# Turning C's queries and keys by 32x32 blocks through memory in a two-layer decoder trunk, with edits to the order of copies, loads and residuals

## The chip, the cores and the metric

One core of a Trainium2 chip runs the whole kernel. Its engines work at the same time, each on its own queue of instructions in program order: TensorE (PE in the profile, PEld its weight loads), VectorE (DVE), ScalarE (ACT), GpSimd (POOL) and SyncE (SP), which here only issues transfers. The metric is the device time of one execution in microseconds (us).

## The reference

Two layers act on a sequence of 256 tokens with 1024 channels, all in float32:

```python
h = h + 0.5 * swiglu(rms_norm(h, g1), w_gate1, w_up1, w_down1)       # D_FF = 2816
u = rms_norm(h, gm);  P = u @ w_in                                   # one wide projection, split by columns
h = h + concat(o_A, o_B, o_C) @ w_out
h = h + 0.5 * swiglu(rms_norm(h, g2), w_gate2, w_up2, w_down2)
```

Group A has 4 query heads on one key head, and each query keeps 64 keys that an indexer scores; with 256 tokens group B (4 heads) is plain causal attention. Both norm queries and keys per head and rotate them. Group C, which the change touches, has 8 heads of 64 channels without rotation, and adds a running sum of log forget gates:

```python
cq = rms_norm(cq, c_q_norm);  ck = rms_norm(ck, c_k_norm)            # per head of 64
s  = cq @ ck.T / 8 + c_sum[query] - c_sum[key]                       # keys up to the query
o_C = softmax(s) @ cv * sigmoid(cg)
```

## The kernel before, in words

**Products.** A float32 product is made of three at full rate: each operand is split into a rounded high part (`h`) and the rest (`l`), and `mm3` adds h·h, h·l and l·h. Weights stream in tiles of 128x1024 that SP fetches (`Weights.load`, L214). `W.pump` splits one tile: ACT casts the high part (`wh`, L273), DVE subtracts for the low one (`wl`, L277). Ten raw tiles and eight split ones can be held. A tile's fetch is issued as soon as an older raw tile has been split, unless `W.hold` is set; `W.free(n)` lifts that and issues up to n at once.

**Feed-forward.** `ffn` runs the hidden columns in chunks of 512. Chunks 2 and 4 go through `seven`, a Strassen-like scheme with seven products of halves in place of eight, whose extra sums are made of copies of PSUM: `keep` (L645) is an ACT copy of a bank that TensorE goes on to write, and `V.tensor_tensor(u4, z, u4)` (L665) reads another such bank. `stepped()` stands between the parts; it runs what is due and pumps two weight tiles. Hidden chunks are turned by DVE in 32x32 blocks (`to_memory`, L474), written to memory, and read back so that the blocks lie in transposed places (`from_memory`, four transfers, L479). The last six rows of w_down are used in `tail` (from L836): for each of four quarters q it finishes `acc[q]`, adds it to the trunk (`residual`, L490) and sends half of the next layer norm's input through memory (`nxt.send`, tile `xd`); `nxt.fetch` reads it back (tile `xT`) and `nxt.rest` splits it (ACT L447, DVE L448). The other half is turned by TensorE (`norm.half`, `turn`, L418).

**Mixer.** The columns of w_in come in eight chunks of four units each, in the order iq, ib, b, a, ck, cq, cv, cg; a unit is 12 matmuls of TensorE. After unit n everything registered by `at_step` with a number up to n runs, sorted by that number, then one tile is pumped. For C, ACT evacuates `ck` and `cq` from PSUM to one SBUF tile (`wide`) and squares them; DVE sums the squares (`c_sums`). At step 25.36 one POOL power takes the root for 32 columns (`head_rs`, L394), and POOL scales the four tiles (`scale_heads`, L947); the gains of both norms are multiplied into cq by POOL (L1228). Group A's selection runs beside it on DVE: eight `topk` rounds at the odd steps from 17 to 31, then `amask` (L1091 to L1095) at step 32. POOL adds the causal mask to the forget rows (L1137).

**A and C heads.** Then AC_ORDER, a list written out by hand, sets the order of all that is left: `s` scores of a pair of heads, `m` mask and row maximum (DVE), `e` exponentials (ACT), `d`/`D` division (DVE or ACT), `f` turning the probabilities on TensorE with an ACT copy out of PSUM, `v` values, `o` output, `q` a half of a w_out product, `w` a pump, `a` a mask add, `T`/`t` turns through memory. `g` is the step of the change: `c_T` turns a pair of C heads by four TensorE transposes of each layer's cq and ck (L1436) and copies the bank to SBUF (ACT, L1437); there are four a layer.

Of the kernel before, what the change touches and what calls it, by code (L numbers as in the profile page):

```python
# [14 lines left out]
ALU = mybir.AluOpType  # L15
# [3 lines left out]
P = 128  # L19
S = 256  # L20
D = 1024
# [15 lines left out]
HELD = 6  # L37
OUT_TAIL = 3
AC_ORDER = """
g2.4 g0.5 s0.01 m0 s1.23 m3 e0 e3 s2.45 D0 q g1.0 a0 m4 m2 e2 q q D3 f0.3 a1 a3 m1 e1 s3.42 s4.01 f3.3  # L40
m5 e4 a2 m6 d2 q g3.5 d1 f2.3 q e5 m7 f1.5 m8 D4 s5.32 t m10 v0.0 w o0 e10 q q q e6 f4.3 q d5 m11 d10
e11 q f5.0 D11 m9 v1.3 T5 o1 v2.2 e8 e7 q D6 w d7 q o2 q e9 q d8 q f6.0 d9 q q w q f7.1 f8.3 f9.2 w v3.0
o3 v5.1 v4.3 o4 w q q
""".split()
# [251 lines left out]
def kernel(ctx: ExitStack, tc: tile.TileContext, x, xt, weights, small, const, out):  # L296
# [184 lines left out]
    def tokens(o, q, hid, w, start, stop, cols=slice(0, 512)):  # L481
# [2 lines left out]
        mm3(o, [h[:, t * P:(t + 1) * P] for h in hid], [v[:, 0, 512 * c + cols.start:512 * c + cols.stop] for v in w],  # L484
            start, stop)

    def residual(q, ps, factor, cols=slice(0, 512)):
        t, c = q % 2, q // 2
        d = trunk[:, t, 512 * c + cols.start:512 * c + cols.stop]
        V.scalar_tensor_tensor(d, ps, factor, d, op0=ALU.mult, op1=ALU.add)  # L490
        return d


    def ffn(norm, nxt, aside=None, first=False):
# [43 lines left out]
            ts = slice(t * P, (t + 1) * P)  # L538
            mm3(ps[t], (norm.h[:, k, ts], norm.l[:, k, ts]), [v[:, k % 2] for v in w], k == 0, k == KT - 1)

        def unit(ps, u):
            w = W.take()
            for k in (2 * u, 2 * u + 1):
                for t in range(2):
                    part(ps, k, w, t)

        def gate(ps, t, n):
            a = tmp(n)
# [79 lines left out]
        def seven(c):  # L628

            def piece(part, t, half):  # L630
                return [part[:, 4 * half + k, t * P:(t + 1) * P] for k in range(4)]

            def form(ps, x, start, stop=False, last=False):
                hs, ls = x if isinstance(x, tuple) else forms[x]
                for u in range(2):
                    w = W.take()
                    for k in range(2):
                        n = 2 * u + k
                        mm3(ps, (hs[n], ls[n]), [v[:, k] for v in w], start and n == 0, stop and n == 3)
                    if not (last and u):  # L640
                        stepped()

            def keep(ps):
                s = tmp(512)
                A.copy(s, ps)  # L645
                return s

            own = lambda t, half: (piece(norm.h, t, half), piece(norm.l, t, half))
            n_down = 1 if c == NC - 1 else 2
            y = bank("gu")  # L650
            form(y, own(0, 0), True)
            s1 = keep(y)
            x = bank("gu")
            form(x, own(0, 1), True, True)
            z = bank("gu")
            form(z, "f3", True)
            form(y, "f2", False, last=True)
            u2 = keep(y)
            stepped()
            for i in range(n_down):  # L660
                down(4 * c - 4 + i)
            V.tensor_tensor(s1, x, s1, op=ALU.add)
            form(y, "f1", False)
            u4 = keep(y)
            V.tensor_tensor(u4, z, u4, op=ALU.add)  # L665
            for i in range(n_down):
                down(4 * c - 4 + n_down + i)
            W.hold = c < NC - 1
            form(y, "f4", False, True)
            W.hold = True  # L670
            a0 = gate([s1, None], 0, 512)
            V.scalar_tensor_tensor(a0, y, minus_r[:, 0:1], a0, op0=ALU.mult, op1=ALU.mult)
            sc = memory(4, "hd")
            to_memory(sc, 0, a0, 4)
            form(z, own(1, 1), False, True, True)
            V.tensor_tensor(u2, z, u2, op=ALU.add)
            a1 = gate([None, u2], 1, 512)
            V.scalar_tensor_tensor(a1, u4, minus_r[:, 1:2], a1, op0=ALU.mult, op1=ALU.mult)
            to_memory(sc, 1, a1, 4)
            last = c == NC - 1  # L680
            if c == at_seven[-1]:
                forms.clear()
                W.home = None
            after(HID_AT, back(4 * c, 4, sc))
            W.free(2 if last else 4)
            W.hold = last
            stepped()
# [75 lines left out]
        for c in range(NC):  # L763
# [4 lines left out]
                continue  # L768
            ps = [bank("gu") for _ in range(2)] if c else g0
            for u in range(0 if c else 2, 4):  # L770
                unit(ps, u)
                if u < 3:
                    stepped()
            if c == 0:
                if first:
                    W.low()
                    norm.sums_T(xT[0])
                A.activation(minus_r, norm.r, AF.Copy, scale=-1.0)
            a = [gate(ps, t, 512) for t in range(2)]
            stepped()  # L780
# [38 lines left out]
            up(a, ps[t][:, S:], t)  # L819
            to_memory(sc, t, a, 2)  # L820
        split = back(4 * NC, 2, sc)
        W.free()
        stepped()
        stepped()
        for k in range(4 * NC - 6, 4 * NC - 4):
# [5 lines left out]
    def tail(acc, rhs, ks, factor, make_norm, late=None, early=()):  # L831
# [12 lines left out]
        if late:  # L844
# [4 lines left out]
            part(2, ks[:1])  # L849
            ahead = [2, 2, 1, 0]  # L850
        if early:
            part(0, ks[:-2])
            early[0]()
            W.pump()
            part(1, ks[:-2])
            for q in range(4):
# [2 lines left out]
                    nxt.half(0, 1)  # L859
                if q == 3:  # L860
                    W.hold = True
                    nxt.rest()
                residual(q, acc[q], factor)
                if q < 2:
                    nxt.send(q, 2, 2)
                else:
                    nxt.send(q - 2, 8 - n_far, n_far)
                nxt.squares(q % 2, q // 2)
                if q == 1:
                    nxt.fetch(2, 2)  # L870
                if q == 2:
                    W.pump()
            W.pump()
# [38 lines left out]
    G.memset(eighth, HD ** -0.5)  # L912

    def mixer(l, norm, nxt):
        room = wide().rearrange("p (n h d) -> p n h d", n=4, h=8)
        cq, ck = ([room[:, 2 * i + t] for t in range(2)] for i in range(2))
        va = [at.tile([P, 8, HD], F32, name=f"va{t}", tag=f"va{t}") for t in range(2)]
        side, count = [], itertools.count()
# [290 lines left out]
        def c_sums(i, dst, ps, when):  # L1209
# [8 lines left out]

            at_step(when, sums)

        def post_ck(ps):
            c_sums(0, ck, ps, 20.76)

        def post_cq(ps):
            c_sums(1, cq, ps, 24.83)
            for t in range(2):
                q = cq[t]
                G.tensor_tensor(q, q, gc[:, None, :].to_broadcast([P, 8, HD]), op=ALU.mult)  # L1228

            def c_norm():  # L1230
                rs = head_rs(c_ss.rearrange("p i t h -> p (i t h)"), 32, "c")
                for t in range(2):
                    for i, d in enumerate((ck, cq)):
                        x = d[t]
                        scale_heads(x, x, rs[:, 16 * i + 8 * t:16 * i + 8 * t + 8])

            at_step(25.36, c_norm)

        hr = sm.tile([P, 2], F32, name="hr", tag="hr")
        at_step(18.32, lambda: V.tensor_scalar(hr, norm.r, 0.5, None, op0=ALU.mult))  # L1240
# [4 lines left out]

        def post_cg(ps):
            spare = xp.tile([P, 4096], F32, name="spare", tag="xhl")
            st["cT"] = spare[:, :2048].rearrange("p (h c s) -> p h c s", h=4, c=2)
            st["sg"] = spare[:, 2048:3072].rearrange("p (i m r) -> p i m r", i=8, m=4)
            st["fmask"].append(spare[:, 3072:3840].rearrange("p (h c) -> p h c", h=2))  # L1250
            st["gate"] = [tmp(512) for _ in range(2)]
# [6 lines left out]
        def run_heads(hs, qk, take, emit=None):  # L1258
            pj, pt, op, sums, bs = {}, {}, {}, {}, {}

            def scores(i):
# [3 lines left out]
                    return  # L1265
                q, k = qk(kind, h)
                bs[i], bs[i + 1] = take(), take()
                for cols, qs, ks in ((slice(0, P), slice(0, P), slice(0, P)),
                                     (slice(P, 3 * P), slice(P, S), slice(0, S))):
                    products((bs[i], bs[i + 1]), cols, q[:, qs], k[:, ks], cols.start == 0)  # L1270

            def masks(i):

# [42 lines left out]
            def flip_pair(i):  # L1316

                d = tab.rearrange("p a b t d -> p (a b t d)")[:, :6 * P]
                blocks([pj.pop(2 * i + e) for e in range(2)], 3, "pd", d.rearrange("p (i x) -> p i x", i=8))
                d = d.rearrange("p (e i b c) -> p e i b c", e=2, i=4, b=3)  # L1320
                for e in range(2):
                    x = d[:, e].rearrange("p i b c -> p b i c")
# [92 lines left out]

        halves = out_halves()

        cT = st["cT"]

        given, banks = [], {}  # L1420

        def take():
# [5 lines left out]
                banks[i] = bank("gu")  # L1428
            return banks[i]

        def c_T(j, copy):

            b = take()
            for c, src in enumerate((cq, ck)):
                for t in range(2):
                    T.transpose(b[:, c * S + t * P:c * S + (t + 1) * P], src[t][:, 2 * j:2 * j + 2], ident)  # L1436
            copy(cT[:, j], b.rearrange("p (c s) -> p c s", c=2))  # L1437

        def blocks(tiles, n, name, to):
            sc = memory(n, name)  # L1440
            for t, x in enumerate(tiles):
                to_memory(sc, t, x, n)
            from_memory(sc, to, nc.sync)

        def turn_gate(_):
            blocks(st["gate"], 4, "gd", st["sg"].rearrange("p i m r -> p i (m r)"))

        def qk_ac(kind, h):
            if kind == "A":
                return st["aqT"][:, h // 2], st["akT"][:, 0]  # L1450
            return cT[:, h // 2, 0], cT[:, h // 2, 1]

        hs = [("A", h) for h in range(4)] + [("C", h) for h in range(8)]
        scores, masks, exps, divide, flip, flip_pair, values, outT = run_heads(hs, qk_ac, take)
        run = dict(q=lambda i: next(halves), w=lambda i: W.pump(), m=masks, e=exps, d=divide, D=lambda i: divide(i, True),
                   T=flip_pair, t=turn_gate,
                   s=lambda i: scores(2 * i), f=flip, F=lambda i: flip(i, V.tensor_copy),
                   g=lambda i: c_T(i, A.copy), G=lambda i: c_T(i, V.tensor_copy),
                   v=lambda i: values(2 * i + 1),
                   o=lambda i: outT(i)(), a=st["add"])  # L1460
        for word in AC_ORDER:
# [67 lines left out]
```

## Time and profile before

| | us |
|---|---|
| median of 3 runs | 979.85 (979.56 to 980.37) |
| the profiled execution, whole | 980.02 |
| its span, first to last instruction | 978.3 |
| PE busy in the span | 970.5 |
| DVE busy | 822.3 |
| ACT busy | 611.2 |
| POOL busy | 167.2 |

The span leaves 1.7 us of the execution outside. Matmuls overlap, so an engine that reads as busy can still lose a slot; where that matters the start times of neighbouring instructions are compared. A matmul with 512 columns starts 0.23 us after the one before when nothing is missing.

### The profile page before, as it was taken

What the parts mean: (1) busy time and instruction counts of PE and PEld (TensorE: products, weight loads), DVE (VectorE), ACT (ScalarE), POOL (GpSimd) and SP (SyncE); (2) the same over time, 40 slices, a digit from 0 to 9 for tenths busy, and PEclk for the clock granted to TensorE, in tenths of its full rate; (3) what the DMA queues carried; (4) which work ended last, traced back from release to release, by engine and by line L of the source; (5) the groups of instructions that cost most, each with busy time, mean ns of one, the idle gap of its engine ahead of it and who ended that gap; (6) DMA issues with size and microseconds to landing.
All of it is one profiled execution on the core that took longest, in us unless ns stands there. A gap on an engine that the chain in (4) does not pass through costs nothing.

```text
span 978.3 us, 13761 instructions
## 1 busy us (share of the span) xinstructions
PE 970.5 (99%) x4608; PEld 801.0 (82%) x4608; DVE 822.3 (84%) x1284; ACT 611.2 (62%) x1024; POOL 167.2 (17%) x190
## 2 busy tenths in 40 slices
PE   9999999999999999999999999999999999999998
PEld 8878878888878888887878888788888788888877
DVE  6999698689987799879679987976899877998794
ACT  6747475567876656547465654756677865575552
POOL 0000002187530000000000000031867200000000
PEclk9999999999999999999999999999999999999999
DMA  9878877675555687768777767877546547687661
GB/s 359 307 196 333 280 257 220 230 263 167 177 192 157 250 228 249 259 195 311 247 276 229 204 243 253 292 234 235 218 155 220 176 146 274 183 300 267 187 240 60
DMA packets 105495, 226.68 MB, mean 232 GB/s; under 512 B 20928, under 2 KB 50896, under 8 KB 105424
## 3 DMA queue, kind: packets, MB, share of 16 engines
q1 hardware_dynamic: 101936, 213.95, 63.0%
q0 software_dynamic: 2304, 8.39, 4.8%
q10 hardware_dynamic: 1184, 3.46, 1.2%
q8 instruction: 36, 0.59, 0.2%
q14 instruction: 35, 0.29, 0.1%
HBM read 208.44 MB, written 17.33 MB: 231 GB/s over the span
## 4 chain that ended last, share of the span: by engine, by line
PE 86%; DVE 5%; DMA 5%; ACT 3%; issue 1%; SPq 1%; ACTq 0%; POOL 0%; DVEq 0%; POOLq 0%
PE ps_gu L383 58%; PE ps_acc L383 25%; DMA xd<-tmp 2%; DVE wl L277 2%; ACT wh L273 2%; DMA hT<-hd 1%; DMA xT<-xd 1%; SPq L479 1%; DVE tmp L474 1%; DMA hd<-tmp 1%; PE ps_gu L1310 1%; PE ps_acc L978 1%; DVE trunk L490 1%; ACT hh L565 0%; DVE tmp L553 0%
## 5 line engine op out<-in xcount | busy, mean ns | idle before, releaser
L383 PE MATMUL ps_gu<-wh,xhl 128*128 128x512 f32 (+2 forms) x1600 | 494.6, 386 | 1.1 <-ACT xhl L447 1.0
L277 DVE TENSOR_TENSOR wl<-raw,wh 128x1024 fp32r<-128x1024 f32 (+2 forms) x340 | 406.5, 1231 | 10.7 <-ACT wh L273 10.3
L273 ACT CAST wh<-raw 128x1024 fp32r<-128x1024 f32 (+2 forms) x340 | 341.0, 1039 | 62.6 <-PE ps_acc L383 20.0
L383 PEld LDWEIGHTS ps_gu<-wh,xhl 128*128 128x128 f32 x1600 | 298.6, 188 | 62.0 <-DVE tmp L665 1.9
L383 PE MATMUL ps_gu<-wl,xhl 128*128 128x512 f32 (+2 forms) x800 | 306.2, 384 | 0.1
L383 PEld LDWEIGHTS ps_gu<-wl,xhl 128*128 128x128 f32 x800 | 150.3, 188 | 28.5 <-DVE wl L277 0.5
L383 PE MATMUL ps_acc<-wh,hh 128*128 128x512 f32 (+1 forms) x352 | 136.6, 388 | 0.0
L383 PE MATMUL ps_acc<-wh,hl 128*128 128x512 f32 (+1 forms) x352 | 136.3, 387 | 0.0
L383 PE MATMUL ps_acc<-wl,hh 128*128 128x512 f32 (+1 forms) x352 | 136.3, 387 | 0.0
L273 ACT CAST wh<-wide 128x1024 fp32r<-128x1024 f32 x48 | 50.0, 1053 | 86.8 <-DVE wide L244 52.5
L242 POOL DMA_DIRECT2D raw<-in_weights_dram x16 | 14.3, 893 | 374.9 <-DVE wide L244 255.2
L383 PEld LDWEIGHTS ps_acc<-wh,hl 128*128 128x128 f32 x352 | 66.1, 188 | 13.5
L383 PEld LDWEIGHTS ps_acc<-wh,hh 128*128 128x128 f32 x352 | 66.1, 188 | 13.5
L383 PEld LDWEIGHTS ps_acc<-wl,hh 128*128 128x128 f32 x352 | 66.1, 188 | 13.4
L277 DVE TENSOR_TENSOR wl<-wide,wh 128x1024 fp32r<-128x1024 f32 x48 | 57.5, 1212 | 5.3 <-ACT wh L273 5.1
L565 ACT CAST hh<-hT 128x256 fp32r<-128x256 f32 x88 | 29.4, 404 | 37.6 <-DMA hT<-hd 37.6
L553 DVE SCALAR_TENSOR_TENSOR tmp<-ps_gu,y_n,tmp 128x512 f32<-128x512 f32 (+1 forms) x32 | 21.3, 667 | 33.7 <-PE ps_gu L383 28.0
L566 DVE TENSOR_TENSOR hl<-hT,hh 128x256 fp32r<-128x256 f32 x88 | 32.0, 424 | 19.0 <-ACT hh L565 19.0
L394 POOL TENSOR_TENSOR y_n<-msq,minus_half 128x2 f32<-128x2 f32 x6 | 7.7, 1288 | 209.1 <-ACT wh L273 153.2
L244 DVE TENSOR_TENSOR wide<-wide,raw 128x1024 f32<-128x1024 f32 x32 | 39.1, 1222 | 0.6
L474 DVE STREAM_TRANSPOSE tmp<-tmp 128x512 f32<-128x512 f32 (+1 forms) x52 | 34.6, 668 | 1.7
L383 PE MATMUL ps_gu<-wh,fp 128*128 128x512 f32 x96 | 33.6, 390 | 0.8 <-ACT tmp L645 0.8
(259 smaller groups left out, 1095.7 us busy)
## 6 DMA issues: line engine op xcount, KB each, us to landing
raw<-in_weights_dram SPq DMA_DIRECT2D x324, 512.0 KB, 5.4
hd<-tmp SPq DMA_DIRECT2D x40, 256.0 KB, 2.0
hT<-hd SPq DMA_DIRECT2D x80, 128.0 KB, 2.6
raw<-in_weights_dram POOLq DMA_DIRECT2D x16, 512.0 KB, 6.6
raw<-in_weights_dram SPq DMA_DIRECT2D x8, 384.0 KB, 4.3
raw<-in_weights_dram SPq DMA_DIRECT2D x8, 336.0 KB, 5.0
raw<-in_weights_dram SPq DMA_DIRECT2D x8, 256.0 KB, 4.5
fmask<-fd ACTq DMA_DIRECT2D x2, 768.0 KB, 8.0
```

The source lines that it names most:

```text
L242: self.nc.gpsimd.dma_start(self.part(*unit), self.kept(rs[0], *unit[1:]), accum_op=ALU.add)
L244: self.nc.vector.tensor_tensor(self.part(*unit), *(self.part(r, *unit[1:]) for r in rs), op=ALU.add)
L273: self.nc.scalar.copy(hv, src)
L277: (engine or self.nc.vector).tensor_tensor(lv, self.srcs[self.n_low], hv.bitcast(F32), op=ALU.subtract)
L383: T.matmul(o, l, r, start=start, stop=stop, skip_group_check=True)
L474: V.transpose(o.rearrange("p (j b c) -> p b j c", j=4, b=n), x.rearrange("p (b j c) -> p b j c", b=n, j=4))
L479: (other if other and j > 1 else eng).dma_start(to[32 * j:32 * j + 32], sc[:, j].rearrange("(i r) x -> r i x", r=32))
L490: V.scalar_tensor_tensor(d, ps, factor, d, op0=ALU.mult, op1=ALU.add)
L553: V.scalar_tensor_tensor(a, u, norm.r[:, t:t + 1], a, op0=ALU.mult, op1=ALU.mult)
L565: A.copy(by(hh), x)
L566: V.tensor_tensor(by(hl), x, by(hh).bitcast(F32), op=ALU.subtract)
L978: T.transpose(ps[:, i * S + t * P:i * S + (t + 1) * P], xs[t][:, (j + i) * P:(j + i + 1) * P], ident)
```

## The change

Queries and keys of C no longer pass TensorE's transposes. `c_turn` sends a tile pair through memory by 32x32 blocks, in the way that hidden chunks go, back into the same part of `wide`. Keys go first: gains into ck, their root (16 columns) at step 21.0, their turn at 24.9. Queries: root at 24.84, turn at 27.9, with weight fetches held from 25.95 until the turn has been issued. Scores read the keys as they lie, with 32-wide runs; the queries of two pairs at a time are copied into order by ACT (`g0`, `g1`). In the feed-forward part the copy out of PSUM comes ahead of the pumps beside it, the first layer's sums of squares are issued half a unit earlier, fetches are held in the tail until the first half of the next norm is on its way, and the last quarter's residual and send come ahead of `nxt.rest`.

```diff
-g2.4 g0.5 s0.01 m0 s1.23 m3 e0 e3 s2.45 D0 q g1.0 a0 m4 m2 e2 q q D3 f0.3 a1 a3 m1 e1 s3.42 s4.01 f3.3
-m5 e4 a2 m6 d2 q g3.5 d1 f2.3 q e5 m7 f1.5 m8 D4 s5.32 t m10 v0.0 w o0 e10 q q q e6 f4.3 q d5 m11 d10
+g0 s0.01 m0 s1.23 m3 e0 e3 s2.45 D0 q g1 a0 m4 m2 e2 q q D3 f0.3 a1 a3 m1 e1 s3.42 s4.01 f3.3
+m5 e4 a2 m6 d2 q d1 f2.3 q e5 m7 f1.5 m8 D4 s5.32 t m10 v0.0 w o0 e10 q q q e6 f4.3 q d5 m11 d10
...
+    def turned(tiles, n, name, to):
+        sc = memory(n, name)
+        for t, x in enumerate(tiles):
+            to_memory(sc, t, x, n)
+        from_memory(sc, to, nc.sync)
@@ unit; the call of the first layer's first chunk gives between=6
+                if k == between:
+                    norm.sums_T(xT[0])
@@ seven
-                    if not (last and u):
+                    if not last or u < 2 - last:
                         stepped()
-            form(y, own(0, 0), True)
+            form(y, own(0, 0), True, last=True)
             s1 = keep(y)
+            stepped()
-            form(y, "f2", False, last=True)
+            form(y, "f2", False, last=2)
             u2 = keep(y)
+            stepped()
             stepped()
-            form(y, "f1", False)
+            form(y, "f1", False, last=True)
             u4 = keep(y)
             V.tensor_tensor(u4, z, u4, op=ALU.add)
+            stepped()
@@ ffn after the last hidden chunk, and tail
-        W.free()
+        W.free(4)
+        W.hold = nxt is not None
...
                 if q == 3:
                     W.hold = True
-                    nxt.rest()
                 residual(q, acc[q], factor)
...
+                if q == 3:
+                    nxt.rest()
                 nxt.squares(q % 2, q // 2)
                 if q == 1:
                     nxt.fetch(2, 2)
+                    W.free(2)
@@ mixer
+        def c_norm(i, d, tag):
+            rs = head_rs(c_ss[:, i].rearrange("p t h -> p (t h)"), 16, tag)
+            for t in range(2):
+                scale_heads(d[t], d[t], rs[:, 8 * t:8 * t + 8])
+        def c_turn(i, d, name):
+            to = wide_room[:, 1024 * i:1024 * i + 1024].rearrange("p (i x) -> p i x", i=8)
+            turned([x.rearrange("p h d -> p (h d)") for x in d], 4, name, to)
+            return to.rearrange("p i (m r) -> p m i r", m=4)
         def post_ck(ps):
             c_sums(0, ck, ps, 20.76)
+            for t in range(2):
+                k = ck[t]
+                G.tensor_tensor(k, k, gc[:, None, :].to_broadcast([P, 8, HD]), op=ALU.mult)
+            at_step(21.0, lambda: c_norm(0, ck, "ck"))
+            at_step(24.9, lambda: st.update(ckT=c_turn(1, ck, "kd")))
         def post_cq(ps):
             c_sums(1, cq, ps, 24.83)
-            for t in range(2):
-                q = cq[t]
-                G.tensor_tensor(q, q, gc[:, None, :].to_broadcast([P, 8, HD]), op=ALU.mult)
-            def c_norm():
-                rs = head_rs(c_ss.rearrange("p i t h -> p (i t h)"), 32, "c")
-                for t in range(2):
-                    for i, d in enumerate((ck, cq)):
-                        x = d[t]
-                        scale_heads(x, x, rs[:, 16 * i + 8 * t:16 * i + 8 * t + 8])
-            at_step(25.36, c_norm)
+            at_step(24.84, lambda: c_norm(1, cq, "cq"))
+            at_step(25.95, lambda: setattr(W, "hold", True))
+            at_step(27.9, lambda: st.update(cqT=c_turn(0, cq, "qd")))
+            at_step(27.9, lambda: W.free(2))
-        def c_T(j, copy):
-            b = take()
-            for c, src in enumerate((cq, ck)):
-                for t in range(2):
-                    T.transpose(b[:, c * S + t * P:c * S + (t + 1) * P], src[t][:, 2 * j:2 * j + 2], ident)
-            copy(cT[:, j], b.rearrange("p (c s) -> p c s", c=2))
+        def c_pairs(j):
+            two = slice(2 * j, 2 * j + 2)
+            A.copy(c_q[:, two].rearrange("p m (i r) -> p m i r", i=8), st["cqT"][:, two])
```

## Rows read from the trace of the kernel before

**Rows 1.** The page, part 1: busy time, share, instructions of each engine.
```profile
PE 970.5 (99%) x4608; PEld 801.0 (82%) x4608; DVE 822.3 (84%) x1284; ACT 611.2 (62%) x1024; POOL 167.2 (17%) x190
```
**Rows 2.** Waits of PEld: waiting group <- released by: us in total, times, longest.
```profile
PEld ps_gu L383 <- ACT tmp L645: 3.4, 5, 1.3
...
PEld ps_gu L383 <- DVE tmp L665: 1.9, 4, 0.5
PEld ps_gu L383 <- ACT xhl L447: 1.8, 2, 1.2
PEld ps_acc L418 <- DVE trunk L490: 1.4, 2, 0.9
...
PEld ps_gu L383 <- DVE wl L277: 0.5, 1, 0.5
```
**Rows 3.** Timeline of PE at three stalls: start, duration, what, [idle before <-releaser].
```profile
68.29 0.39 PE L383 MATMUL ps_gu<-wh,fpT 128*128 128x512 f32 x1
69.52 0.50 PE L383 MATMUL ps_gu<-wh,fp 128*128 128x512 f32 x1 [0.84 <-ACT tmp L645]
69.86 0.40 PE L383 MATMUL ps_gu<-wl,fp 128*128 128x512 f32 x1
...
493.33 0.50 PE L383 MATMUL ps_gu<-wh,xhl 128*128 128x512 f32 x1 [0.74 <-ACT xhl L447]
...
670.91 0.44 PE L418 MATMUL ps_acc<-ident,trunk 128*128 128x128 f32 x2 [0.70 <-DVE trunk L490]
```
**Rows 4.** Chain of waits between the second and third feed-forward: start, us, what.
```profile
482.46 6.53 DMA xd<-tmp
...
495.57 1.96 DMA xd<-tmp
```
**Rows 5.** Timeline of SP ahead of the first of these writes: start, us, transfers, count.
```profile
474.03 5.85 SPq L214 DMA_DIRECT2D raw<-in_weights_dram  x8
```
**Rows 6.** Chain of waits, first transposes of layer one's A/C stage.
```profile
276.46 0.87 PE ps_acc L1436 x8
```
**Rows 7.** Timeline of DVE, end of the first mixer's projection to the gate's turn.
```profile
266.49 1.21 DVE L277 TENSOR_TENSOR wl<-raw,wh 128x1024 fp32r<-128x1024 f32 x1
...
267.96 1.73 DVE L277 TENSOR_TENSOR wl<-raw,wh 128x1024 fp32r<-128x1024 f32 x1
...
273.58 2.69 DVE L1093 SCALAR_TENSOR_TENSOR amask<-score,cst 128x128 f32<-128x128 f32 x2
...
278.32 0.35 DVE L1284 CUSTOM_DVE_ANT_0 tmp<-ps_gu,amask,minus_a 128x128 f32<-128x128 f32 x1 [0.52 <-PE ps_gu L383]
...
286.70 1.28 DVE L474 STREAM_TRANSPOSE tmp<-tmp 128x512 f32<-128x512 f32 x2
```
**Rows 8.** Timeline of POOL, same stretch.
```profile
253.52 1.97 POOL L394 TENSOR_TENSOR y_a<-ssa,minus_half 128x10 f32<-128x10 f32 x1 [13.18 <-DVE sums L1300]
...
260.57 6.37 POOL L394 TENSOR_TENSOR y_c<-c_ss,minus_half 128x32 f32<-128x32 f32 x1 [1.25 <-DVE c_ss L393]
267.02 6.56 POOL L947 TENSOR_TENSOR wide<-wide,y_c 128x512 f32<-128x512 f32 x4
273.54 2.58 POOL L1137 TENSOR_TENSOR fmask<-fmask,causal 128x512 f32<-128x512 f32 x2
```
**Rows 9.** Transfers of the gate's turn (tile gd), writes and reads together.
```profile
DMA to landing us min/median/max: 2.0/2.6/3.1
```
**Rows 10.** Timeline of ACT, first A/C stage.
```profile
278.71 0.40 ACT L1293 ACTIVATE p<-tmp,nm 128x128 f32<-128x128 f32 x1 [0.56 <-DVE nm L1284]
...
283.24 0.46 ACT L1312 COPY pT<-ps_gu 128x384 f32<-128x384 f32 x1
...
285.84 0.57 ACT L1437 COPY spare<-ps_acc 128x512 f32<-128x512 f32 x1
```
**Rows 11.** Stretches: busy us of PE, PEld, DVE, ACT, POOL; granted clock, DMA share, GB/s.
```profile
270.00:275.00 5.00, 5.00 (x24) 4.14 (x23) 5.00 (x9) 2.11 (x2) 5.00 (x5) 1.00 0.98 348
...
280.00:285.00 5.00, 5.00 (x37) 3.95 (x36) 3.87 (x26) 5.00 (x20) 2.54 (x2) 1.00 0.20 76
```

More of the change, by code (lines that the diff above doesn't have):

```diff
@@ L539, in part, with unit @@
             mm3(ps[t], (norm.h[:, k, ts], norm.l[:, k, ts]), [v[:, k % 2] for v in w], k == 0, k == KT - 1)
-        def unit(ps, u):
+        def unit(ps, u, between=None):
             w = W.take()
@@ L770, in ffn @@
             for u in range(0 if c else 2, 4):
-                unit(ps, u)
+                unit(ps, u, 6 if first and not c else None)
                 if u < 3:
@@ L851, in tail @@
         if early:
+            W.hold = True
             part(0, ks[:-2])
@@ L914, in mixer @@
     def mixer(l, norm, nxt):
-        room = wide().rearrange("p (n h d) -> p n h d", n=4, h=8)
+        wide_room = wide()
+        room = wide_room.rearrange("p (n h d) -> p n h d", n=4, h=8)
         cq, ck = ([room[:, 2 * i + t] for t in range(2)] for i in range(2))
@@ L1247, in post_cg @@
             spare = xp.tile([P, 4096], F32, name="spare", tag="xhl")
-            st["cT"] = spare[:, :2048].rearrange("p (h c s) -> p h c s", h=4, c=2)
+            st["cq"] = spare[:, :1024].rearrange("p (m s) -> p m s", m=4)
             st["sg"] = spare[:, 2048:3072].rearrange("p (i m r) -> p i m r", i=8, m=4)
@@ L1267, in scores @@
                 bs[i], bs[i + 1] = take(), take()
-                for cols, qs, ks in ((slice(0, P), slice(0, P), slice(0, P)),
-                                     (slice(P, 3 * P), slice(P, S), slice(0, S))):
-                    products((bs[i], bs[i + 1]), cols, q[:, qs], k[:, ks], cols.start == 0)
+                for cols, qs, n in ((slice(0, P), slice(0, P), P), (slice(P, 3 * P), slice(P, S), S)):
+                    some = k[:, :n] if len(k.shape) == 2 else k[:, :n // 32]
+                    products((bs[i], bs[i + 1]), cols, q[:, qs], some, cols.start == 0)
             def masks(i):
@@ L1318, in flip_pair @@
                 d = tab.rearrange("p a b t d -> p (a b t d)")[:, :6 * P]
-                blocks([pj.pop(2 * i + e) for e in range(2)], 3, "pd", d.rearrange("p (i x) -> p i x", i=8))
+                turned([pj.pop(2 * i + e) for e in range(2)], 3, "pd", d.rearrange("p (i x) -> p i x", i=8))
                 d = d.rearrange("p (e i b c) -> p e i b c", e=2, i=4, b=3)
@@ L1416, in mixer @@
         halves = out_halves()
-        cT = st["cT"]
         given, banks = [], {}
@@ L1429, in take @@
             return banks[i]
-        def c_T(j, copy):
-            b = take()
-            for c, src in enumerate((cq, ck)):
-                for t in range(2):
-                    T.transpose(b[:, c * S + t * P:c * S + (t + 1) * P], src[t][:, 2 * j:2 * j + 2], ident)
-            copy(cT[:, j], b.rearrange("p (c s) -> p c s", c=2))
[L1439 to L1443, printed above, removed]
+        c_q = st["cq"]
+        def c_pairs(j):
+            two = slice(2 * j, 2 * j + 2)
+            A.copy(c_q[:, two].rearrange("p m (i r) -> p m i r", i=8), st["cqT"][:, two])
         def turn_gate(_):
-            blocks(st["gate"], 4, "gd", st["sg"].rearrange("p i m r -> p i (m r)"))
+            turned(st["gate"], 4, "gd", st["sg"].rearrange("p i m r -> p i (m r)"))
         def qk_ac(kind, h):
@@ L1450, in qk_ac @@
                 return st["aqT"][:, h // 2], st["akT"][:, 0]
-            return cT[:, h // 2, 0], cT[:, h // 2, 1]
+            return c_q[:, h // 2], st["ckT"][:, h // 2]
         hs = [("A", h) for h in range(4)] + [("C", h) for h in range(8)]
         scores, masks, exps, divide, flip, flip_pair, values, outT = run_heads(hs, qk_ac, take)
-        run = dict(q=lambda i: next(halves), w=lambda i: W.pump(), m=masks, e=exps, d=divide, D=lambda i: divide(i, True),
+        run = dict(q=lambda i: next(halves), w=lambda i: W.pump(), m=masks, e=exps, d=divide, D=lambda i: divide(i, True), g=c_pairs,
                    T=flip_pair, t=turn_gate,
                    s=lambda i: scores(2 * i), f=flip, F=lambda i: flip(i, V.tensor_copy),
-                   g=lambda i: c_T(i, A.copy), G=lambda i: c_T(i, V.tensor_copy),
                    v=lambda i: values(2 * i + 1),
```

1 line of the change is left out of this document (removed).

## The prediction

> **What bounds the kernel now.** I read the page's first part first: TensorE is busy nearly the whole span, DVE 84%, ACT 62% [rows 1]. So only two things can shorten it: instructions that leave TensorE, and its lost slots. The waits of its weight loads come second, as they name those slots: 3.4 us on the ACT copy L645, 1.9 on the sum L665, 1.8 on the split L447, 1.4 on the residual L490, 0.5 on wl [rows 2]. The timeline shows what a wait costs: from 68.29 to 69.86 two slots take 1.57 us where two times 0.23 would do, so a wait of 1.3 loses 1.1 [rows 3]. The chain of waits third: between the second and third feed-forward it runs through one write of `xd` of 6.53 us, while the next write of the same kind takes 1.96 [rows 4]. Last the A/C stage: there TensorE is full and ACT is too, 5.00 of 5.00 us from 280 to 285, but the first exponential waits for DVE's row maximum, and that for the first scores [rows 7, 10, 11]. Three engines meet there.
>
> **Transposes that leave TensorE.** Eight take 0.87 us in the chain [rows 6], 0.11 each. Four `c_T` of four in two layers are 32: 3.5 us of the bound engine. This is the gross gain. How much remains is decided at two places of the A/C stage.
>
> First the start, which hangs on DVE's `m0`. It begins at 278.32 after 0.52 of idleness, released by the scores [rows 7]. Eight transposes stood ahead of these scores, so they come 0.87 earlier, and DVE must be ready for that. But DVE gets four transposes of 128x512 a layer, 0.64 each from the pair of 1.28 [rows 7]: 2.6 us between step 25 and `m0`, behind the same weight splits and topk rounds. Against that stands what POOL stops doing late. Now it takes 6.37 for a root of 32 columns and 6.56 for four scalings, to 273.58, then adds masks for 2.58 [rows 8]. A weight split that takes 1.21 ahead of the scalings takes 1.73 beside them, and two ops of 128x128 take 2.69 beside the mask add, though a 128x1024 op takes 1.21 [rows 7]: some 2.2 of it is waiting. The Trainium skill states why (GPSIMD Engine Reference, Specifications): GpSimd's SBUF interfaces are shared with VectorE, and contention is with ops that have two SBUF inputs or a two-port mode. By that rule the splits suffer and the new transposes don't; the two rows agree for the first, and no row shows the second.
>
> In the new order the keys' root and scalings fall into POOL's idle 13.18 us [rows 8]. A root of 16 columns lies between 1.97 (10) and 6.37 (32), on their line 3.2; two scalings are 3.3. So cq is ready about 260.6 + 6.5 = 267, where DVE comes to its turn after about 1.3 more work than now: a wait of 0 to 1. The masks of A, 2.6 later, fall mostly behind the mask add's end at 276.1, so the 2.2 and the 0.5 go, and perhaps 1.0 comes back where the keys' scalings meet other DVE work. Sum for `m0`: +2.6 - 2.7 + 1.0, less the idle 0.5: +0.4. The bounds are -0.9 (the scores' whole advance) and +2.1 (no relief from POOL: 2.6 - 0.5). I take +0.4, since the rows show the relief directly but not the new meeting.
>
> Second, ACT. Two of the four copies of `g` stay as copies from SBUF; I count them as equal to those from PSUM (0.57), with at worst twice that, which would cost 0.6 a layer. The one of `g3`, 0.57 at 285.84 [rows 10], goes, in the stretch where ACT is full. Before it, the next block of transposes (f3.3) needs the bank that ACT copies until 283.70 [rows 10], so TensorE's 1.3 us of advance there meets a chain that starts with `m0` and is lost. After it, about 0.6 is kept. Net a layer: +0.4 - 0.6 = -0.2, both layers **-0.4**, with ends of -1.75 a layer (sixteen times 0.11) and +1.5.
>
> **The turn through memory.** The gate's turn stands for it. Its writes and reads land in 2.0 to 3.1 [rows 9]; with 1.3 for DVE's pair, 2.2 for the writes, four issues on SP at no more than 0.7 each (eight fetches took 5.85 [rows 5]; I take 2.0) and 2.6 for the reads that is 8.1 from first transpose to last landing. From 267 it ends at 275.1; the scores of C's first pair follow the start that the transposes have now, 276.46 [rows 6], by sixteen short matmuls of A, some 1.6 us, so the copy `g0` (0.6) may begin until 277.4: 2.3 us of slack, and a little more before it holds up the exponentials behind it on ACT (278.71 [rows 10]). The fetches held from 25.95 on are there to keep it so, as the DMA share is 0.98 from 270 to 275 and 0.20 from 280 to 285 [rows 11]: what is deferred has room later. SP's queue stands still behind each turn for some 5 us, and the weight fetches behind it. Ten raw tiles of one unit each (12 slots, 2.7 us) cover that. The keys' turn has four units and more, and costs no wait. The wider use of `wide` until the last scores delays no one before the next feed-forward's second chunk.
>
> At this point a rule of the Trainium skill speaks against the change (VectorE: DVE Perf Modes, Rules for kernel authors): transpose a 128x128 tile on TensorE where PSUM will do, with VectorE only for 32x32 blocks. By it the turn is no gain; the rows say that TensorE's 0.11 each is time on the bound engine and DVE's 0.64 is not, unless `m0` waits, which is the third rival below.
>
> **`seven`.** The copy L645 comes ahead of two or four pumps that now precede it in ACT's queue, and L665 ahead of two. Waits: 3.4 in five and 1.9 in four [rows 2], less 0.2 each for the slot (1.3 against 1.1): 2.4 and 1.1. Behind the moved copies the casts come 0.6 later, the low parts 0.7. Where these are next in line, part returns; I leave out half of the longest, 0.5: **-3.0**, with bounds -3.5 and 0.
>
> **Boundaries.** Now eight fetches are issued just ahead of `xd` [rows 5]; with at most four, the 6.53 should come near 1.96 [rows 4]; the first half then lands some 4 us sooner, and the last residual no longer waits in DVE's queue behind `rest`. The waits on L447, L490 and wl are 3.7 together [rows 2]; less 0.2 for each of five they are 2.7. I take **-2.9**, between the two, as the moved residual is due when the last quarter ends, which is ahead of all three. What comes late next would be `rest` itself behind the residual and its transpose (1.4 more on DVE), about half a microsecond ahead of its use; and the four fetches that are held, for tiles some seven units away. Bounds: -3.7 and 0. The earlier sums of squares in the first chunk only let ACT start sooner; TensorE doesn't wait there: 0, between -0.3 and +0.1.
>
> **Sum.** -0.4 - 3.0 - 2.9 = -6.3 against the profiled execution's 980.02 (span 978.3 and 1.7 around it): 973.7. The median lies 0.17 lower: **973.5**.
>
> **Rivals.**
> *TensorE alone sets the A/C stage.* If DVE is ready 0.9 sooner, all 3.5 us of transposes count: from the median 979.85 - 3.5 - 5.9 = 970.4. For it: TensorE shows no idle there [rows 11]. Against it: ACT is as full. Chance 0.17.
> *The stalls move but don't go*: the copies' place is taken by casts that come later, held fetches arrive late. A third of 5.9 is left: 979.85 - 0.4 - 2.0 = 977.5. Chance 0.10.
> *DVE pays for the turn*: no relief from POOL, `m0` later by 2.1, ACT gives 0.6 back: +1.5 a layer; 979.85 - 5.9 + 3.0 = 977.0. For it: DVE shows idle before `m0` of only 0.52 [rows 7]. Against it: POOL is done 6.5 us sooner. Chance 0.14. (This is where the Trainium skill's rule on transposes, above, would come true.)
> *Slower: the queries' turn lands too late.* Its writes share the rings with the forget rows and any fetch issued before the hold. If a write takes 6.5 as behind eight fetches [rows 4] and the reads 5 instead of 2.6, `g0` is 6.9 late, 4.6 after the slack, in each layer: 979.85 - 5.9 + 9.2 = 983.2. It decides from 3 us past the slack per layer, where the gains are eaten. Against it: the hold stands exactly there. Chance 0.07.
> The forecast, 971.8 to 975.5, has 0.50; 0.02 is for anything else.
>
> **Chances.** Differences under 0.2% (2 us) can't be told from none. Faster: the forecast, the first rival, most of the second and third: 0.83. Same: the rest of these, 0.09. Slower 0.08. The range reaches from 969.5 to 978.0: the forecast, the first rival and most of the cases near 977.
>
> **What would show it.** Right: no transposes of `wide` on PE; waits on L645 and L665 near 0; `xd` writes near 2 to 3 at all three boundaries; `m0` within 1 us of now relative to the end of the projection, with DVE ops beside POOL shorter at the end and longer at the keys' scalings; POOL's root near 3.2. Wrong: a PE or ACT wait on the queries' turn, `m0` released by a late `amask`, or new waits on wl and wh behind the moved copies. The forecast falls if the A/C stage grows by over 2 us a layer or if the boundaries keep their waits.

## The result, and the profile after

The changed kernel takes 992.23 us (median of 6 runs, 988.36 to 993.29), the kernel before beside it 980.11: ratio 1.0115, interval 1.0094 to 1.0136. It is slower by 12 us; the forecast was 973.5, with a range from 969.5 to 978.0, so faster. The profiled execution took 991.86, span 990.1, mean granted clock 0.993 where it was 1.000 before.

First the page's first part, which answers to [rows 1]:

```profile
PE 973.5 (98%) x4576; PEld 802.1 (81%) x4576; DVE 824.5 (83%) x1294; ACT 609.5 (62%) x1020; POOL 162.2 (16%) x192
```

The 32 transposes are gone, yet TensorE is busy longer. The waits of the weight loads (group <- released by: us in total, times, longest), which answer to [rows 2], say what came in:

```profile
PEld ps_acc L383 <- ACT spare L1455: 9.9, 2, 5.4
PEld ps_acc L1332 <- DVE p L1327: 3.5, 2, 1.8
...
PEld ps_gu L383 <- ACT xhl L447: 0.9, 1, 0.9
```

The waits on the `seven`'s copy and sum and on the residual are no longer in this view, that on L447 is halved: what the feed-forward edits were to remove is removed. New are 9.9 us on ACT's copy of the turned queries (`g0`) and 3.5 us on DVE's divisions. PE's timeline of layer one (start, us, what, [idle before <-releaser]) shows the first:

```profile
284.02 1.72 PE L383 MATMUL ps_acc<-wide,spare 64*128 64x128 f32 x8 [4.96 <-ACT spare L1455]
...
286.69 0.63 PE L383 MATMUL ps_acc<-wh,ol 128*128 128x512 f32 x1
...
288.73 0.39 PE L383 MATMUL ps_acc<-wl,oh 128*128 128x512 f32 x1
```

Behind the pause a product of 512 columns takes 0.63, later 0.39. The windows (us, then busy us of PE, PEld, DVE, ACT, POOL; granted clock, DMA share, GB/s) give the cause: TensorE's clock falls from 2.4 to 1.2 GHz in the pause and is back by 290 (granted clock 0.50 in every microsecond from 282 to 288).

```profile
280.00:285.00 5.00, 0.98 (x6) 0.98 (x8) 1.04 (x7) 1.65 (x6) 2.50 (x2) 0.68 0.94 331
285.00:290.00 5.00, 5.00 (x22) 3.43 (x21) 2.67 (x18) 3.79 (x14) 0.00 (x0) 0.64 1.02 418
290.00:295.00 5.00, 5.00 (x40) 3.59 (x40) 4.15 (x21) 4.37 (x18) 0.00 (x0) 1.00 0.12 47
```

The chain of waits (start, us, what) leads back from that pause:

```profile
267.09 1.30 DVE tmp L474 x2
...
268.41 7.54 DMA qd<-tmp
...
277.43 5.85 DMA wide<-qd
```

The queries are ready at 267.09, where the prediction had 267. Then a write takes 7.54 to its landing, where the gate's transfers took 2.0 to 3.1 [rows 9], and the last read 5.85. Who is beside them is on ACT's and SP's timelines:

```profile
266.31 0.37 ACTq L1147 DMA_DIRECT2D fmask<-fd  x1
266.72 0.45 ACTq L1147 DMA_DIRECT2D gmask<-fd  x1
...
277.40 0.36 ACTq L1147 DMA_DIRECT2D spare<-fd  x1
```

```profile
261.37 0.92 SPq L475 DMA_DIRECT2D kd<-tmp  x2
264.18 1.98 SPq L479 DMA_DIRECT2D wide<-kd  x4
...
267.81 0.91 SPq L475 DMA_DIRECT2D qd<-tmp  x2
276.08 1.80 SPq L479 DMA_DIRECT2D wide<-qd  x4
277.99 5.68 SPq L214 DMA_DIRECT2D raw<-in_weights_dram  x7
```

ACT spreads the forget rows over the partitions (768, 384 and later 384 KB) 1.5 us ahead of the queries' writes, and seven fetches of 512 KB follow the reads at once.

The second new wait stands on POOL's and DVE's timelines, where the keys' scaling comes beside the division of B's heads:

```profile
253.13 2.05 POOL L962 TENSOR_TENSOR wide<-wide,y_ck 128x512 f32<-128x512 f32 x2
...
274.02 3.54 POOL L1152 TENSOR_TENSOR fmask<-fmask,causal 128x512 f32<-128x512 f32 x2 [7.94 <-DMA fmask<-fd]
```

```profile
253.09 2.24 DVE L1327 TENSOR_SCALAR p<-p,sums 128x128 f32<-128x128 f32 x2
...
256.58 0.55 DVE L1327 TENSOR_SCALAR p<-p,sums 128x128 f32<-128x128 f32 x2
```

Two divisions of the same shapes take 2.24 beside the scaling and 0.55 behind it, and the flips of B wait for them.

Matching TensorE's instructions one by one in both traces gives the account in us (layer one, layer two): flips of B +1.4, +1.4; eight transposes gone -0.6, -0.6; the pause +5.3, +4.5; the slow clock behind it +1.3, +2.2. All the rest, opening included, is -3.0. Together +11.9: the last product starts at 974.76 before, at 986.61 after.

### The profile page after: what moved, and what is told of

Same layout as the page of the kernel before. It is cut to its first block, busy times and chain, and to the rows that moved or that the text cites. A ratio compares the mean times of both kernels' runs of the same rounds, so it can differ in the third digit from the quotient of the medians.

```text
span 990.1 us, 13758 instructions
## 1 busy us (share of the span) xinstructions
PE 973.5 (98%) x4576; PEld 802.1 (81%) x4576; DVE 824.5 (83%) x1294; ACT 609.5 (62%) x1020; POOL 162.2 (16%) x192
## 4 chain that ended last, share of the span: by engine, by line
PE 89%; DVE 4%; DMA 3%; ACT 2%; issue 1%; SPq 0%; POOL 0%; ACTq 0%; POOLq 0%
PE ps_gu L383 58%; PE ps_acc L383 29%; DVE wl L277 1%; DMA qd<-tmp 1%; PE ps_gu L1332 1%; DMA wide<-qd 1%; DMA spare<-fd 1%; DMA xd<-tmp 1%; PE ps_acc L993 0%; DMA hd<-tmp 0%; ACT wh L273 0%; PE ps_acc L418 0%; DVE tmp L474 0%; DVE p L1327 0%; SPq L479 0%
```

## Experiments

Theory: the queries' turn lands late because other transfers share its rings; the pause costs the clock on top; the keys' scaling holds the divisions; the edits outside the mixer gain. Rivals: those edits lose too; the turn is slow of itself; DVE and the strided keys pay. Each ratio below is against the kernel before, timed beside the run at 981.0 to 981.2.

**The parts alone.** First the change without its mixer part. Its expectation says that the tail's edits stay; this kernel had the tail's hold, but not its release and not the `rest` moved behind the sends.

```
 (mixer as before; of the tail:)
         if early:
+            W.hold = True
```

> The change without its mixer part: queries and keys of C are turned by TensorE as before, with one root and scale for both; the edits in the two feed-forward blocks, the `sevens`, the tail and the holds stay. Theory A (the whole loss lies in the mixer, the other edits gain what the prediction gave them): span and time fall by 4.5 to 6 us against before, about 974 to 975.5, and the granted clock is 1.00 in both A/C stages. Theory B (the feed-forward edits lose too, for instance by later fetches): 978 or more.

Measured 983.98, ratio 1.0035 (1.0019 to 1.005): slower, as theory B has it. The chain at the boundary of the feed-forward blocks shows why:

```profile
495.51 6.23 DMA raw<-in_weights_dram
...
502.79 0.51 ACT xhl L447
...
503.35 6.72 PE ps_gu L383 x16
```

With the hold and no release, the next fetches stand behind the last half's reads; ACT waits 6.2 us for one with a weight cast that is ahead of the norm's copy in its queue. TensorE stands still meanwhile, and its granted clock is 0.75 from 500 to 505 and 0.56 from 505 to 510. The complement, the kernel before with the mixer part and those two tail edits:

```
 (seven, sums of the first chunk, tail's hold as before; mixer changed; of the tail:)
+                    W.free(2)                 (q == 1)
+                    nxt.rest()                (q == 3, behind the send)
```

> The kernel before with the mixer part of the change alone. Theory A: the loss of the changed kernel (+12 us) and the gain of the rest (-5 to -6) add, so this stands at +16 to +18 us, about 996 to 998, with a PE pause of 4.5 to 5.5 us in each layer ahead of the first C scores. Theory B (the parts work on each other, the feed-forward edits shift the fetches under the queries' writes): +8 us or less.

Measured 996.77, ratio 1.0164 (1.0139 to 1.0189): theory A, the loss is in the mixer. Then all edits outside it, with the release:

```
 (mixer as before; the rest of the change, and with it:)
+            W.hold = True
+                    W.free(2)                 (q == 1)
+                    nxt.rest()                (q == 3, behind the send)
```

> All edits of the change outside the mixer: the sums of the norm, the seventh products, the tail with its hold AND its release and with the far rest behind the sends (the release and the far rest were left out of the earlier kernel without the mixer part). Theory A (these edits gain, the loss is the mixer's): 974 to 976.5; the boundary of the two feed-forward blocks at 495 to 505 us costs no more than the 3.3 us it cost before. Theory B (the boundary edits are worth nothing or lose, as with the hold alone, where ACT waited 6.2 us for a late fetch there): 979 or more.

Measured 976.42 beside 981.08, ratio 0.995 (0.9934 to 0.9966), clock 1.000: -4.7 us (by the interval -3.3 to -6.5), theory A. With the hold but neither its release nor the moved `rest` the edits lose 3.0 us, with both they gain; which of the two makes the difference was not run.

**What makes the turn late.** The first two spreads earlier on ACT:

```
-SUMS_STEP, MASK_STEP = ..., 22.33, 29.63
+SUMS_STEP, MASK_STEP = ..., 22.33, 26.5
```

> The changed kernel with the two spreads of the forget rows (768 and 384 KB, issued on ACT) at step 26.5 in place of 29.63, so ahead of the queries' writes. Theory A (the writes are slow because they share the rings with these spreads): the two writes land 2.3 to 3.5 us after their issue in place of 7.5, the reads start at about 271 in place of 276.1 and land before 279, the pause of 5 us ahead of the first C score and the fall of the clock behind it go: -5 to -6.5 us a layer, 979 to 982. Theory B (writes are slow of themselves, or wait behind the weight fetch at 266.3): the landing stays at 6 us or more and the time within 2 us of 992. Theory C (DVE and the strided keys pay, the wait is only a sign of it): writes land early, but the time stays above 988.

Measured 994.34, ratio 1.0145 (1.0118 to 1.0172): no gain. The time alone speaks for theory B; SP's timeline says more:

```profile
262.00 0.92 SPq L475 DMA_DIRECT2D kd<-tmp  x2
268.55 2.62 SPq L479 DMA_DIRECT2D wide<-kd  x4
...
271.71 0.91 SPq L475 DMA_DIRECT2D qd<-tmp  x2
277.16 1.80 SPq L479 DMA_DIRECT2D wide<-qd  x4
```

The spreads were issued at 262.1, beside the keys' writes. These now take the blow: their reads start 6.6 us after the writes' issue instead of 2.8, and the queries' writes queue behind them on SP to 271.7. Once issued they land in 4.7 us in place of 7.5, though not in the 2.3 to 3.5 of theory A. The contention moved one turn up.

Then the fetches behind the reads, held by a small store that needs `g0`:

```
-            at_step(27.9, lambda: W.free(2))
+g0 b s0.01 ...        b: nc.sync.dma_start(mark, c_q[0:1, 0]); W.free(7)
```

> The changed kernel with the seven weight fetches that stand right behind the queries' reads put behind a 1 KB store on the same queue that has to wait for ACT's first copy of the turned queries. Theory A (the reads are slow because 3.6 MB of fetches share their rings): the reads land 2 to 3 us after the last issue at 277.9, so at 280 to 281 in place of 283.3; -2.5 to -3.5 us a layer, 985 to 987. Theory B (the reads are slow of themselves): they land at 283 as before and the time stays at 992, or 993 to 995 because the fetches come 4 us later.

Measured 989.76, ratio 1.008 (1.0052 to 1.0109): -2.5 against 992.23, less than theory A gave and not clear of the spread, as the two intervals overlap. By the matched products the pause goes from 5.3 to 4.9 us in layer one and from 4.5 to 3.1 in two. In layer one the last read still lands at 283.4, as theory B has it, 4.95 after its issue in place of 5.85. The transfers issued from 276 to 279 (KB each, median us to landing) show what was still there:

```profile
wide<-qd SPq DMA_DIRECT2D x4, 128.0 KB, 3.0
spare<-fd ACTq DMA_DIRECT2D x1, 384.0 KB, 4.9
```

The third spread is in flight beside these reads too. So all spreads on SP, two behind the queries' reads, the third behind the fetches:

```
-            A.dma_start(m, bass.AP(tensor=rows_.tensor, ...        (in spread)
+            nc.sync.dma_start(m, bass.AP(tensor=rows_.tensor, ...
-            at_step(MASK_STEP, mask_tiles)
+            at_step(27.95, mask_tiles)     and W.free(2) at 27.96
```

> The changed kernel with the three spreads of the forget rows issued on SP: two right behind the queries' reads and ahead of the freed fetches, the third behind the fetches. So from 267.8 on the queries' writes share the rings with one weight fetch only, and their reads with none of ACT's spreads. Theory A (the turn is late since these transfers share its rings): writes land within 4 us, by 272; the last read lands by 276, ahead of the first C score at 278.7; the pause (5.3 and 4.5 us) and the low clock behind it (1.5 to 2 us a layer) go: 977 to 981. Theory B (the turn takes its 15 us whatever stands beside it): 990 or more. Theory C (the wait goes but DVE, the strided keys or the later masks hold the C scores up instead): 983 to 989.

Measured 996.53, ratio 1.0151 (1.0122 to 1.018). The time misses by 16 us, but the part in question came out as theory A has it:

```profile
266.92 0.91 SPq L475 DMA_DIRECT2D qd<-tmp  x2
270.19 1.80 SPq L479 DMA_DIRECT2D wide<-qd  x4
...
273.00 4.43 SPq L214 DMA_DIRECT2D raw<-in_weights_dram  x7
```

The reads start 3.3 us after the first write's issue instead of 8.3, and TensorE waits for the queries in neither layer. One weight fetch stands right ahead of the writes here (265.21) as in the changed kernel (266.32), so this alone did not hold them up. A new wait took the place, 14.0 us in the two layers; its chain:

```profile
278.86 11.14 DMA spare<-fd
...
290.14 1.26 POOL spare L1152
291.40 1.23 POOL gmask L1152
```

The third spread stands behind 3.6 MB of fetches, POOL adds its mask ahead of the second one, and the C heads wait.

**The keys' scaling**, on top of that kernel:

```
-B_TURN, A_ROPE, ... = 18.83, 19.48, ...
+B_TURN, A_ROPE, ... = 18.83, 18.98, ...
```

> As the run with the spreads behind the reads, and A's rope half a step earlier, so that POOL has done it ahead of the keys' gains and scales the keys before 252 in place of 253.1 to 255.1. Theory A (POOL's scaling holds DVE's divisions of B, 2.24 in place of 0.55 us, and these the flips by 1.35 us): the PE wait at 256 us goes, 1.2 to 1.5 us a layer less than that run, 974 to 978. Theory B (the divisions are late for another reason, or the scaling then blocks other DVE work in the same chain): within 0.8 us of that run.

Measured 995.23, ratio 1.014 (1.011 to 1.0171): by time inconclusive. In the trace the scaling is at 249.36; the two divisions at 253.85, which met it before, take 0.55, and two earlier ones that meet it now take 1.34:

```profile
250.28 1.34 DVE L1327 TENSOR_SCALAR p<-p,sums 128x128 f32<-128x128 f32 x2
253.85 0.55 DVE L1327 TENSOR_SCALAR p<-p,sums 128x128 f32<-128x128 f32 x2
```

**The clock.**

```
-m3 e0 e3 s2.45 D0        +m3 e0 e3 x s2.45 D0
+        x: for i in range(20): mm(acc[0][:, :P], ones, ones, i == 0, i == 19)
```

> The changed kernel with 20 products of 128x128 with ones (some 4.3 us, their result is overwritten) ahead of the first C scores, where TensorE stands still for 5.0 and 4.5 us. Theory A (the pause itself takes the clock away, and that costs 1.5 to 2 us a layer on top): the wait for the queries stays, the granted clock behind it is 1.00, and the time falls by 3 to 4 us, to 988 to 989. Theory B (the slow stretch behind the pause is DMA or ACT work that came late, not the clock): the clock stays high or not, the time within 1 us of 992.

Measured 990.72, ratio 1.0097 (1.0072 to 1.0123), mean clock 1.000. The wait for the queries stays, and the clock is full throughout (window 285 to 290):

```profile
285.00:290.00 5.00, 4.97 (x36) 3.73 (x36) 3.05 (x21) 5.00 (x19) 1.61 (x2) 1.00 1.03 416
```

Matched with the changed kernel, TensorE makes good 2.1 and 2.6 us behind the pause. Its C scores start 1.0 and 0.6 later than there, which takes part of it back; the fillers are not the reason, as they end at 283.99 and TensorE still waits 1.04 us for `g0`, so the queries themselves came later in this run. The clock and the matched products are as theory A has them. The time is not: 1.5 us below 992.23 is inside the spread of the runs, and theory A gave 3 to 4.

**Placing the transfers.** The third spread ahead of five of the fetches:

```
+            def some(): W.free(3); W.hold = True
-            at_step(27.96, lambda: W.free(2))
+            at_step(27.96, some)
             spread(st["fmask"][3], 6)
+            W.free(5)
```

> As the run with the spreads behind the reads, but the third spread stands on SP ahead of five of the seven freed fetches, not behind all (there it landed 11.1 us after its issue, at 290, and POOL, which adds the third mask before the second, and TensorE at 287.8 waited 6.4 us for it). Theory A (that one late spread is all that was left of the loss): it lands before 281, TensorE's wait at 287.8 goes, and each A/C stage stands 1 us or more ahead of the kernel before: 974 to 977, 5 us below before. Theory B (another transfer or DVE's masks hold the C heads up behind it): 980 or more.

Measured 983.85, ratio 1.0027 (1.0015 to 1.0038), clock 1.000: 12.7 below the run with the spreads behind the reads, so the late spread was most of that loss, but in theory B's range: something else still holds the C heads up. And with the rope earlier:

> The same with A's rope half a step earlier, so that POOL scales the keys before 252 and not beside DVE's divisions of B (two of them took 2.32 us beside it, 0.64 us else). Theory A (the wait of the flips at 256 us is worth its full size, some 0.8 us a layer): 1 to 2 us below the run without it, 972.5 to 976. Theory B (the flips' wait is made good by the wait for ACT or for the top-k behind it): within 0.5 us of that run.

Measured 982.32, ratio 1.0015 (1.0001 to 1.0028): 1.5 us below. That is theory A's difference, over twelve runs each; its absolute 972.5 to 976 rested on the run before and is missed. In the traces the first flip at 256 us comes 1.2 earlier than in that run. The chain names what is left:

```profile
273.12 5.98 DMA gmask<-fd
279.12 1.31 POOL fmask L1152
...
286.87 0.44 PE ps_acc L1337 x2
```

The second spread lands at 279.1, behind the queries' turn. Both spreads need the forget rows only, which are in memory by 252, so:

```
-            at_step(27.95, mask_tiles)
+            at_step(23.4, mask_tiles)
```

> As the run with the rope earlier, but the first two spreads (768 and 384 KB) stand on SP at step 23.4, behind the landing of the forget rows and ahead of the keys' writes, so in the stretch from 252 to 260 where the rings were busy to 0.47. The keys' turn, the queries' turn, then two fetches, the third spread and the other fetches follow. Theory A (what is left of the loss is the second spread, landing at 279.1 behind the queries' turn, for which POOL's mask addition, DVE's C masks and the flip at 286.9 wait): the waits from 279 to 287 go, each A/C stage ends 1 us or more ahead of the kernel before, 973 to 976, below the run without the turn of queries and keys (976.4). Theory B (the spreads now delay the keys' turn or a weight fetch in 252 to 262 and the wait returns there): 978 or more. Theory C (the turn by memory is worth nothing once nothing waits for it, since its transposes cost what they replace): 976 to 978.

Measured 975.89 (974.72 to 977.78) beside 981.2, ratio 0.995 (0.9934 to 0.9966), span 973.9: the time that theory A gave. SP's timeline shows every transfer in a place of its own:

```profile
252.26 0.34 SPq L1147 DMA_DIRECT2D fmask<-fd  x1
...
259.30 0.91 SPq L475 DMA_DIRECT2D kd<-tmp  x2
262.05 2.28 SPq L479 DMA_DIRECT2D wide<-kd  x4
...
265.74 0.91 SPq L475 DMA_DIRECT2D qd<-tmp  x2
269.83 1.80 SPq L479 DMA_DIRECT2D wide<-qd  x4
271.73 0.87 SPq L214 DMA_DIRECT2D raw<-in_weights_dram  x2
275.69 0.33 SPq L1147 DMA_DIRECT2D spare<-fd  x1
```

On ACT's timeline and in the windows nothing waits for the queries any more:

```profile
276.29 0.61 ACT L1460 COPY spare<-wide 128x512 f32<-128x512 f32 x1
...
275.00:280.00 5.00, 5.00 (x36) 3.88 (x36) 4.27 (x22) 4.93 (x15) 0.00 (x0) 1.00 0.97 279
```

This version beats the kernel before, the only one with the turn that does. By time it can't be told from the one without it (976.42), so theory C stays open. By the traces its mixers, from the first transposes of the norm to the first product that reads the paired flip, take 115.76 us in either layer, without the turn 116.53 and 117.28: 0.8 and 1.5 us less. Not all of this need be the turn's. The rope and the spreads stand elsewhere too, which was not run without the turn, and 0.8 of layer two's 1.5 comes at the last of these products, where the run without the turn waits for the paired flip's read.

## Why the prediction was wrong

- **Transposes that leave TensorE (-0.4).** Gone as said, 1.75 us a layer. What they can leave behind may have been underrated for a turn that is not late: the last version's mixers are 0.8 and 1.5 us shorter than those without the turn, where the prediction had 0.2, but that difference holds the moved rope and spreads as well.
- **`m0` (+0.4).** In layer one it starts at 279.49 where it started at 278.32, with A's scores on TensorE within 0.02 of their old place: +1.2. The relief was to come from POOL being done early. POOL was, but its mask addition waited 7.94 us for a spread and still ran from 274.02 to 277.56, beside `amask` (1.31 for one op at 276.34). The pause hid it.
- **"Perhaps 1.0 comes back where the keys' scalings meet other DVE work."** It came back as 1.7 on the divisions, and these stand ahead of TensorE: +1.4 a layer. The prediction priced the meeting on `m0`, not where it happens.
- **The turn through memory: the step that failed.** The start (267), DVE's 1.3 and the 2.0 for SP's issues were right. The writes took 7.5 us where the sum has 2.2, and the last read 5.9 where it has 2.6, so the end was 283.3 and not 275.1. The gate's turn stood for transfers of the same shape, but it goes out in another stretch (287.4, where the DMA share is 0.30), and the share of 0.98 from 270 to 275 [rows 11] was read as weight fetches, which the hold defers. A good part of it was the forget rows' spreads, which ACT issues and no hold touches: in that stretch ACT's queue moved 0.79 of 1.74 MB, and with the fetches held the share is still 0.94. The trace of before has them (starts in layers one and two; landing of all transfers of the forget rows):

```profile
L1132 ACTq DMA_DIRECT2D fmask<-fd x2: 332/344/356, 265.5 to 750.6; - x2
...
DMA to landing us min/median/max: 3.7/8.3/10.1
```

  So the row that speaks for lateness was in view, and "the hold stands exactly there" argued from a line's position and not from what was on the rings. The hold is also undone right behind the reads. The Trainium skill has the rule (DMA: Bandwidth & Descriptors, Queues, rings and completion order): SP and ACT own one queue row each on the same engines, which go round between rows packet by packet. The runs agree: the writes take 7.2 to 8.2 us beside ACT's spreads and 2.6 to 4.0 in the runs with the spreads behind or ahead of both turns.
- **The slower rival** had the right mechanism at a chance of 0.07: it gave `g0` 6.9 us late (its terms, 6.5 - 2.2 and 5 - 2.6, add up to 6.7) and 4.6 after the slack; the pause was 5.3 and 4.5. It left out the clock (+1.3 and +2.2) and the divisions (+1.4 twice), which make up most of the way from its 983.2 to 992.23.
- **`seven` (-3.0) and boundaries (-2.9).** Alone they gave -4.7 of -5.9, which the interval doesn't tell from the full sum. The waits on the copy and the sum are gone. The boundary term looks too large: matched product by product they give 0.1, 1.2 and 0.9 us in the changed kernel and 0.5, 0.0 and 0.9 in the run of these edits alone, of 2.9. Between the feed-forward blocks a write of `xd` still takes 4.96 after the change (before 6.53 [rows 4]), and 0.9 of the wait on L447 stays.

```profile
498.09 4.96 DMA xd<-tmp
```

- **TensorE alone sets the stage; DVE pays for the turn.** Neither can be judged from the changed kernel. In the last version `g0` runs at 276.29 without a wait, TensorE is busy 5.00 of 5.00 in every window from 270 to 290, and its mixers gain 0.8 and 1.5 of the gross 1.75, with the reservation above.

What stays open: how much the turn is worth in time, since 0.5 us between the two best versions is below what these runs tell apart, and no run has the last version's rope and spreads without the turn.

## What to carry to other kernels

A turn through memory is two trips, so price it with what is on the rings at that moment, from every queue, and not with the same turn elsewhere: list the transfers issued within some 10 us before its first write and behind its last read. A hold on one queue says nothing about another's; a transfer whose data are ready early should go where the rings are idle (here the places of three spreads, with the rope half a step earlier, separated 996.5 from 975.9). And when a wait is removed and the time stays, read the next link before calling the theory wrong: in two runs here (the spreads behind the reads, and that with the rope earlier) the links under test behaved as the right theory said, and the time hid it.

## What the runs showed of the hardware that was not expected

- A pause of TensorE of 4 to 5 us cost 2.1 to 2.6 us more behind it: products of 512 columns at 0.63 instead of 0.39 us, granted clock 0.64 from 285 to 290; with fillers in the pause it stayed 1.00.
- An elementwise DVE op with one tensor input from SBUF (division of 128x128 and 128x256, 0.55 for the two) takes 2.24 beside POOL's scaling, but 0.55 beside POOL's root (253.85 to 254.40 in the run with the spreads behind the reads and the rope earlier, root of 10 columns from 253.83; 250.31 to 250.86 in the changed kernel, root of 16 columns from 250.13 to 253.04). The Trainium skill (GPSIMD Engine Reference, Specifications) names two kinds of DVE ops that contend with GpSimd: with two SBUF inputs, or in a two-port mode. The first is not this one; the 2.24 may be the second, which no row shows, and the roots' rows show that POOL's op matters as well.
- A broadcast of 384 KB landed in 4.9 us beside four small reads, and in 11.1 us behind 3.6 MB of fetches on its own queue.
